# Weight sums by adding transfers: part of the weight preparation of a feed-forward stage moved from VectorE to transfers that GpSimd issues

## The chip, the cores and the metric

The kernel runs on one core of one Trainium2 chip. The metric is the device time of one execution in microseconds (us). Before the change it is 1514.25 us, the median of 2 runs (1512.74 and 1515.76).

## The reference

The program is one inference step of a two-layer transformer on 640 tokens: 512 latent tokens and 128 prompt tokens, with 1024 features each. Layer 0 mixes tokens with latent attention and neighbourhood attention, layer 1 with grouped-query attention. Each layer ends with a gated feed-forward stage of width 2816. All of it is in 32-bit floats.

```python
D_MODEL = 1024
D_FF = -(-8 * D_MODEL // (3 * 256)) * 256        # 2816

def swiglu(h, w_in, w_out):
    gate, up = jnp.split(h @ w_in, 2, axis=-1)
    return (jax.nn.silu(gate) * up) @ w_out

def reference(...):
    for l in range(DEPTH):                        # DEPTH = 2
        ...
        xp = xp + g1_p * out_p
        xs = xs + g1_s * out_s
        hp = modulate(rms_norm(xp, norm_ffn[l]), sh2_p, sc2_p)
        hs = modulate(rms_norm(xs, norm_ffn[l]), sh2_s, sc2_s)
        xp = xp + g2_p * swiglu(hp, w_ffn_in[l], w_ffn_out[l])
        xs = xs + g2_s * swiglu(hs, w_ffn_in[l], w_ffn_out[l])
```

The change concerns `h @ w_in` of layer 1: the products with the gate and up weights.

## The kernel before

**Arithmetic.** Operands of TensorE are split in two parts: a rounded high part (type fp32r) and the low part, which is the difference from the full value. A product of two split operands is three matmuls: high by high, high by low, low by high. ScalarE makes the high part of a weight tile by a copy into the fp32r type, VectorE the low part by a subtraction.

**The feed-forward stage.** `ffn(l, ...)` walks over 22 blocks of 128 of the 2816 columns. Each block fb has an up tile u and a gate tile g in memory, `wFI[l, fb, 1]` and `wFI[l, fb, 0]`, each 128 x 1024 values or 512 KB: eight pieces of 128 input features side by side, of which the first four (the left half) and the last four (the right half) are the two halves of the inner dimension. Tokens are split in two halves of 320 too. From block 2 on, gate and up of a block are computed together as a two by two block product with seven instead of eight half-products (a scheme of Strassen's kind). This needs sums of weight halves beside the weights:

- X is u itself.
- Y is s13: left half g left + g right, right half u left + g left.
- Z is s24: left half s13 right + g right, right half s24 left + u right.
- W is the right half of g.

A block makes seven half-products, each of 4 pieces by 3 matmuls, so 84 matmuls of 128x128 by 128x320. In order they are X with "11", Y with "D", W with "E" (this one belongs to the block before, the `job`), Z with "N", X with "21", Z with "22", Y with "C". The first, E, N and C write a bank g, D and 22 a bank b5, 21 a bank b2. ScalarE copies out what is in g after the first product (p1), after N (u1), and b5 after D (p5). VectorE adds these up.

**Weights ahead.** In block fb the weights of n = fb + 1 are prepared, by a class `Weights`: `sums` makes s13 and s24 in four VectorE additions of 128 x 512, `hi("X")`, `hi("Y")`, `hi("Z")` and `hi_w` the high parts on ScalarE, and `lo(...)` and `lo_w` the low parts on VectorE. The split tiles X, Y and Z take turns in six places. s13 and s24 share a tag "ws" with two places. The raw u tiles share three places with the `wm` tiles (weights of a modulation that VectorE works off in some of the blocks), the raw g tiles have two.

**What sets the order.** Nearly all VectorE work of the loop is issued through `dve` and all ScalarE work through `act`, two objects that tie each instruction behind the one issued before, so each of the two engines keeps the order of the code. The order of the transfers is not tied like that. A planner lays out the queues: a load is put where its place comes free, so that u(fb + 3) is issued in block fb, while the code names `fetch_u(fb + 2)` there. All transfers of this loop go through the queue of SyncE: u, g, `wm`, and the spills, by which finished blocks (7 tiles of 320 KB for a pair of blocks) are parked in memory. GpSimd has nothing to do in the second layer's blocks. In the trace most instructions of the loop carry the line of the helper `dve`/`act` (L1097), and all matmuls L62, so they are told apart by tile names (s is s13 or s24, wX, wY and wZ the split tiles, "wu" and "wg" the raw ones, p and u ScalarE's copies p1, p5 and u1; lead and sg the activations, hd the split activations on their way to the spills).

The stage exists for both layers; `paired` is true for layer 1.

Of the kernel before, what the change touches and what calls it, by code (L numbers as in the profile page):

```python
# [11 lines left out]
F32 = mybir.dt.float32  # L12
F32R = mybir.dt.float32r
AF = mybir.ActivationFunctionType
ALU = mybir.AluOpType
# [3 lines left out]
P = 128  # L19
# [8 lines left out]
FB = DFF // P  # L28
# [21 lines left out]
def body(ctx, tc, xT, vecs, crow, wm0, wm0g, wm1, wA, wNV, wNA, wMK, wMV, wOA, wGQ, wGK, wGV, wOC,  # L50
         wFI, wFO, cckvT, ckrT, cnkT, cnv, cgkT, cgv, rpbp, tabM, tabK, tabG, maskN,
         yT, o_ckvT, o_krT, o_nkT, o_nv, o_gkT, o_gv):
    nc = tc.nc
    V, S, G = nc.vector, nc.scalar, nc.gpsimd
# [32 lines left out]
    def bank(name, kind="m"):  # L87
        if kind == "m":
            return psp.tile([P, 512], F32, tag="m", bufs=4, name=name)
        return ypool["pool"].tile([P, 512], F32, tag=kind, bufs=ypool["tags"][kind], name=name)  # L90
# [10 lines left out]
    def tmp(name):  # L101
        return tp.tile([P, T], F32, tag="t", bufs=3, name=name)

    def f(ap):
        return ap.bitcast(F32)
# [55 lines left out]
    def load(src, n, name):  # L161
        raw = rawp.tile([P, 1024], F32, tag="raw", name=name)
        nc.sync.dma_start(raw[:, :n], src)
        return raw[:, :n]

    def after(inst, fn):
        if inst is None:
            return fn()
        with tc.issue_after(inst.ins):
            return fn()  # L170
# [901 lines left out]
    def ffn(l, x, pend, hm, nxt, side, opened):  # L1072
        ph, fk, dr, hd, fs, fp, w0, _ = opened
        paired = l == 1
# [5 lines left out]
        def room():  # L1080
            place[0] += 1
            return hd[(place[0] - 1) % len(hd)]
# [3 lines left out]
        def wtile(name):  # L1086

            turn[0] += 1
            return (wp, fp)[turn[0] % 2].tile([P, 2, 1024], F32R, tag="w", bufs=3, name=name)
# [10 lines left out]
        dve, act = Line(), Line()  # L1100


        def high(t, src):
            act(S.activation, t[:, 0, :], src, AF.Copy)

        def low(t, src):
            dve(V.tensor_tensor, t[:, 1, :], src, f(t[:, 0, :]), ALU.subtract)

        def two(t):
            return t[:, 0, :], t[:, 1, :]  # L1110
# [5 lines left out]
        def product(ps, wt, w0, which, first):  # L1116
            for k, (h, l_) in enumerate(hm.operand(which)):
                a, b = [w[:, w0 + k * P:w0 + k * P + P] for w in wt]
                mm3(ps[:, :HT], a, b, h, l_, first and k == 0, k == 3, skip_group_check=not first)

        def utile(name):
            return tp.tile([P, HT], F32, tag="u", bufs=7, name=name)
# [3 lines left out]
        def spill(fb, dh, dl):  # L1126
            if fb < FB - STAY:
                spilt[fb] = []
                for t, c in ((dh, "h"), (dl, "l")):
                    d = dr.tile([P, T], F32, name=f"sp{l}_{fb}{c}")  # L1130
                    nc.sync.dma_start(d, f(t))
                    spilt[fb].append(d)
            else:
                kept[fb] = dh, dl
# [34 lines left out]
        def fetch_u(fb):  # L1169
            if fb < FB:  # L1170
                raws[fb] = [load(wFI[l, fb, 1], 1024, f"wu{l}_{fb}r")]

        def fetch_g(fb):
            if fb == FEW:
                raws[fb].append(load(wFI[l, fb, 0], 1024, f"wg{l}_{fb}r"))
            elif fb < FB:
                rg = fp.tile([P, 1024], F32, tag="wr", bufs=2, name=f"wg{l}_{fb}r")
                nc.sync.dma_start(rg, wFI[l, fb, 0])
                raws[fb].append(rg)

        class Weights:

            def __init__(self, fb):
# [3 lines left out]

            def sums(self):
                ru, rg = self.u, self.g
                s13 = fp.tile([P, 1024], F32, tag="ws", bufs=2, name=f"s13{l}_{self.fb}")  # L1190
                dve(V.tensor_tensor, s13[:, :512], rg[:, :512], rg[:, 512:], ALU.add)
                dve(V.tensor_tensor, s13[:, 512:], ru[:, :512], rg[:, :512], ALU.add)
                s24 = fp.tile([P, 1024], F32, tag="ws", bufs=2, name=f"s24{l}_{self.fb}")
                dve(V.tensor_tensor, s24[:, :512], s13[:, 512:], rg[:, 512:], ALU.add)
                dve(V.tensor_tensor, s24[:, 512:], s24[:, :512], ru[:, 512:], ALU.add)
                self.s = {"X": ru, "Y": s13, "Z": s24}
                self.t = {c: wtile(f"w{c}{l}_{self.fb}") for c in "XYZ" if c != "X" or self.X is None}

            def hi(self, c):
                if c in self.t:  # L1200
                    high(self.t[c], self.s[c])

            def lo(self, c):
                if c in self.t:
                    low(self.t[c], self.s[c])
                    setattr(self, c, two(self.t[c]))

            def hi_w(self):
# [108 lines left out]
        for fb in range(FEW, FB):  # L1317

            first = fb < FEW + AHEAD
            n = Weights(fb + 1) if fb < FB - 1 else None  # L1320
            b5 = bank(f"fd{l}_{fb}")
            up = tmp(f"up{l}_{fb}")
            sg = lead if paired and PAIR_OF.get(fb, (0, 1))[1] == 0 else tmp(f"sg{l}_{fb}")
            both = paired and job and job[0] in PAIR_OF
            p5, u1, g2 = [utile(f"{c}{l}_{fb}") for c in ("p5", "u1", "g2")]
            if n:
                n.sums()
            if n and not first:
                n.hi("X")
            if fb in early:  # L1330
                g = early[fb][0]
            else:
                g, b2, p1 = bank(f"fg{l}_{fb}"), bank(f"fu{l}_{fb}", "y"), utile(f"p1{l}_{fb}")
                product(g, w.X, 0, 11, True)
                act(S.activation, p1, g[:, :HT], AF.Copy)
            if n and not first:
                n.hi("Y")
                n.lo("X")
                n.hi("Z")
                n.lo("Y")  # L1340
                fetch_u(fb + 2)
            after(PE.last, lambda: product(b5, w.Y, 0, "D", True))
            act(S.activation, p5, b5[:, :HT], AF.Copy)
            if n and not first:
                n.lo("Z")
            if job:
                jb, jg, jW, jup, jsg = job
                product(jg, jW, 0, "E", False)
                if jb in early:
                    dve(V.tensor_tensor, jsg[:, HT:T], jup[:, HT:T], jsg[:, HT:T], ALU.mult)  # L1350
                act(S.activation, jsg[:, 0:HT], jg[:, :HT], AF.Silu, scale=-1.0)
                if jb in early:
                    dve(V.tensor_tensor, jsg[:, 0:HT], early[jb][1], jsg[:, 0:HT], ALU.mult)
                else:
                    dve(V.tensor_tensor, jsg, jup, jsg, ALU.mult)
            if n and not first:
                n.hi_w()
            if both:
                split_pair(jb, jsg, 0)
            elif job:  # L1360
                dh, dl = room(), room()
                act(S.activation, dh, jsg, AF.Copy)
            product(g, w.Z, 0, "N", False)
            act(S.activation, u1, g[:, :HT], AF.Copy)
            if n:
                if first:
                    for c in "XYZ":
                        n.hi(c)
                        n.lo(c)
                    fetch_u(fb + 2)  # L1370
                    n.hi_w()
                n.lo_w()
                fetch_g(fb + 2)
            if both:
                split_pair(jb, jsg, 1)
            elif job:
                dve(V.tensor_tensor, dl, jsg, f(dh), ALU.subtract)
                spill(jb, dh, dl)
            if fb not in early:
                product(b2, w.X, 512, 21, True)  # L1380
                dve(V.tensor_tensor, up[:, 0:HT], b2[:, :HT], p1, ALU.add)
            if both:
                split_pair(jb, jsg, 2)
            step("fb", fb, dve)
            step("load", fb + 1, act)
            product(b5, w.Z, 512, 22, False)
            dve(V.tensor_tensor, up[:, HT:T], b5[:, :HT], u1, ALU.add)
            product(g, w.Y, 512, "C", False)
            dve(V.tensor_tensor, g2, g[:, :HT], p5, ALU.add)
            act(S.activation, sg[:, HT:T], g2, AF.Silu, scale=-1.0)  # L1390
            job, w = (fb, g, w.W, up, sg), n
# [69 lines left out]
        pss, ws = {}, {}  # L1461
# [43 lines left out]
        if paired:  # L1505
# [51 lines left out]
            for c, i in [(c, i) for c in ("T4", "T1", "B22") for i in range(len(PAIRS))][len(more):]:  # L1557
                tag = spots.pop(0)
                fetch_kind(c, i, *((fo, "hd") if tag == "fo" else (ring, tag)))
            for p in range(4):  # L1560
# [3 lines left out]
                for k, (c, which, to) in enumerate(PLAN):  # L1564
                    j = p * len(PLAN) + k
# [121 lines left out]
    ws = [unit(wGK[v], 1024, f"wgk{v}") for v in range(2)]  # L1687
# [366 lines left out]
```

## Time and profile before

| | |
|---|---|
| Time, median of 2 runs | 1514.25 us |
| Time of the profiled execution | 1513.06 us |
| Its span, from first to last instruction | 1511.3 us |
| Mean granted TensorE clock | 0.992 |
| TensorE busy | 1455.6 us, 96% of the span |
| VectorE busy | 1191.1 us, 79% |
| ScalarE busy | 760.1 us, 50% |
| GpSimd busy | 224.6 us, 15% |
| Blocks 5 to 20 of layer 1, from 1142.6 to 1339.5 us | 196.9 us, TensorE busy 196.9, VectorE 189.1, ScalarE 107.4, GpSimd 0 |
| Read from memory and written to it | 191.18 MB and 34.68 MB |

The profile is one execution. An engine's busy time counts only its own work, not waiting, and not the issuing of transfers. A share over the whole span mixes stages, so for the blocks a line of their own is given. A transfer has an issue, on the queue of an engine, and a landing some us later; only the landing releases who waits for it.

### The profile page before, as it was taken

Reading aid. Unit: us, or ns where it says so; the run is one execution under the profiler, and the core shown is the slowest. Engines: PE = TensorE matmul, PEld = TensorE weight load, DVE = VectorE, ACT = ScalarE, POOL = GpSimd, SP = SyncE. Lnnn points to the kernel's source line nnn. Section 1 sums busy time; section 2 is a strip of 40 time slices with the busy share of each in tenths; the row PEclk is TensorE's granted clock in tenths of the full one; section 3 lists DMA queues with packets and bytes.
Section 4 is the critical chain, followed back from the end, with each engine's and each line's share of the span. In section 5 each row is a group of like instructions: output and inputs, shape, how many; then the busy total and the mean of one; then the engine's idle time right before and its main releaser. Section 6 shows DMA issues by size and latency. Waiting matters only on the chain.

```text
span 1511.3 us, 25796 instructions
## 1 busy us (share of the span) xinstructions
PE 1455.6 (96%) x9856; PEld 1401.0 (93%) x9856; DVE 1191.1 (79%) x2234; ACT 760.1 (50%) x1501; POOL 224.6 (15%) x295
## 2 busy tenths in 40 slices
PE   5999989989999999999999999999999999999996
PEld 4888878879999999999999889989999999999996
DVE  5646686885899999977997777784899999953486
ACT  5435576773656554441123656673655555542242
POOL 0225544431100000000001433221200000000000
PEclk9999999999999999999999999999999999999998
DMA  9324541005155555569763210012145556669531
GB/s 373 107 104 137 184 151 46 29 15 167 57 172 184 178 185 184 179 209 332 276 218 130 90 46 29 29 57 79 57 170 185 177 191 209 214 213 313 181 95 70
DMA packets 79723, 227.54 MB, mean 151 GB/s; under 512 B 8832, under 2 KB 14224, under 8 KB 79344
## 3 DMA queue, kind: packets, MB, share of 16 engines
q1 hardware_dynamic: 77552, 222.54, 43.0%
q10 hardware_dynamic: 1632, 2.43, 0.5%
q8 instruction: 77, 1.26, 0.3%
q0 software_dynamic: 416, 0.93, 0.2%
q14 instruction: 46, 0.38, 0.1%
HBM read 191.18 MB, written 34.68 MB: 149 GB/s over the span
## 4 chain that ended last, share of the span: by engine, by line
PE 84%; DVE 8%; ACT 4%; DMA 2%; issue 2%; POOL 0%; DVEq 0%; SPq 0%; ACTq 0%; POOLq 0%
PE fg L62 20%; PE fd L62 9%; PE fo L62 7%; PE fu L62 6%; PE gq L62 2%; PE nq L62 2%; PE nk L62 2%; PE fo_2b L62 1%; PE fo_0b L62 1%; DMA mraw<-in_wm 1%; PE go L62 1%; PE fo_2a L62 1%; PE fo_0a L62 1%; PE mod L62 1%; PE ms L62 1%
## 5 line engine op out<-in xcount | busy, mean ns | idle before, releaser
L1645 DVE SCALAR_TENSOR_TENSOR junk<-wm,cb 128x1024 bf16<-128x1024 f32 x62 | 75.6, 1219 | 7.1 <-DMA wm<-in_wm 6.6
L1097 ACT ACTIVATE sg<-g 128x320 f32<-128x320 f32 x34 | 16.1, 472 | 115.0 <-DVE g L1097 115.0
L251 POOL TENSOR_SCALAR h10h<-h10t,gs,mods 128x320 fp32r<-128x320 f32 x4 | 3.6, 888 | 429.5 <-DVE h10t L245 427.8
L62 PE MATMUL gq<-h10h,wgq 128*128 128x320 f32 x256 | 65.7, 315 | 0.5 <-DVE gb L1828 0.3
L1097 DVE SCALAR_TENSOR_TENSOR junk<-wm,cb 128x1024 bf16<-128x1024 f32 x50 | 61.0, 1220 | 0.8
L1097 DVE TENSOR_TENSOR wY<-s,wY 128x1024 fp32r<-128x1024 f32 x40 | 48.8, 1219 | 2.2 <-ACT wY L1097 2.2
L1097 DVE TENSOR_TENSOR wZ<-s,wZ 128x1024 fp32r<-128x1024 f32 x40 | 48.7, 1219 | 0.0
L62 PEld LDWEIGHTS gq<-h10h,wgq 128*128 128x128 f32 x256 | 44.7, 188 | 1.8 <-PE gtp L66 1.3
L1097 ACT ACTIVATE wZ<-s 128x1024 fp32r<-128x1024 f32 x40 | 42.4, 1060 | 0.1
L1097 ACT ACTIVATE wY<-s 128x1024 fp32r<-128x1024 f32 x40 | 42.0, 1049 | 0.0
L1829 ACT ACTIVATE gp<-gs,gb,rq 128x640 f32<-128x640 f32 (+1 forms) x40 | 31.9, 797 | 20.0 <-DVE gb L1828 15.9
L62 PE MATMUL gq<-h10l,wgq 128*128 128x320 f32 x128 | 39.4, 308 | 0.0
L62 PE MATMUL fg<-h11E,wW 128*128 128x320 f32 x240 | 38.7, 310 | 0.0
L62 PE MATMUL fg<-h01q,wX 128*128 128x320 f32 x240 | 38.6, 309 | 0.0
L62 PE MATMUL fg<-h11q,wX 128*128 128x320 f32 x240 | 38.6, 309 | 0.0
L62 PE MATMUL fg<-h01N,wZ 128*128 128x320 f32 x240 | 38.6, 309 | 0.0
L62 PE MATMUL fg<-h11N,wZ 128*128 128x320 f32 x240 | 38.6, 309 | 0.0
L62 PE MATMUL fu<-h11q,wX 128*128 128x320 f32 x240 | 38.6, 308 | 0.0
L62 PE MATMUL fu<-h01q,wX 128*128 128x320 f32 x240 | 38.6, 309 | 0.0
L62 PE MATMUL fg<-h01E,wW 128*128 128x320 f32 x240 | 38.6, 309 | 0.0
L62 PE MATMUL fd<-h01q,wZ 128*128 128x320 f32 x240 | 38.5, 309 | 0.0
L62 PE MATMUL fg<-h11C,wY 128*128 128x320 f32 x240 | 38.5, 309 | 0.0
(3209 smaller groups left out, 5257.5 us busy)
## 6 DMA issues: line engine op xcount, KB each, us to landing
wm<-in_wm SPq DMA_DIRECT2D x48, 512.0 KB, 3.9
mraw<-in_wm SPq DMA_DIRECT2D x24, 512.0 KB, 3.6
mraw<-in_wm SPq DMA_DIRECT2D x8, 1024.0 KB, 15.3
hr_T<-sp_T SPq DMA_DIRECT2D x21, 320.0 KB, 5.7
hr_B<-sp_B SPq DMA_DIRECT2D x18, 320.0 KB, 6.0
wm<-in_wm0g SPq DMA_DIRECT2D x8, 512.0 KB, 3.4
x<-in_xT SPq DMA_DIRECT2D x8, 320.0 KB, 5.6
xr<-in_xT SPq DMA_DIRECT2D x8, 320.0 KB, 6.0
```

The lines of the kernel that those rows point to most:

```text
L62: cls.last = nc.tensor.matmul(*a, **k)
L251: G.tensor_scalar(h[:, c0:c1], t, self.gsl[:, k, 0:1], self.ml[:, self.sh + k, 0:1], ALU.mult, ALU.add)
L1097: self.last = after(self.last, lambda: op(*a, **k))
L1645: def step(kind, at, line=lambda op, *a, **k: op(*a, **k)):
L1829: S.activation(dst, src, AF.Exp, bias=nb, scale=rq[:, j:j + 1], accum_out=ll[:, j:j + 1])
```

## The change

In layer 1, for blocks 7 to 21:

- s13 is no longer made by two VectorE additions. A new function `fetch_s(fb + 2)`, called in block fb ahead of `fetch_u(fb + 2)`, loads the left half of g and the left half of u into the two halves of an s13 tile, by two transfers of 256 KB on SyncE's queue. Two more transfers of 256 KB, issued by GpSimd, add the right half of g and the left half of g at their destination.
- The low part of X is no longer made by VectorE's subtraction. ScalarE writes the negated high part into the place of the low part, as one more `act` right behind `hi("X")`, and a transfer of 512 KB, issued by GpSimd, adds the raw u from memory to it.

The raw tiles of u and g are still loaded, for X's high part, for s24 and for W. s13 keeps its tag "ws" with two places, which it shares with s24.

```diff
+        ADDED = 6
+        summed = {}
+
+        def fetch_s(fb):
+            if paired and ADDED < fb < FB:
+                s13 = fp.tile([P, 1024], F32, tag="ws", bufs=2, name=f"s13{l}_{fb}")
+                for j in range(2):
+                    nc.sync.dma_start(s13[:, 512 * j:512 * j + 512], wFI[l, fb, j][:, :512])
+                for j in range(2):
+                    nc.gpsimd.dma_start(s13[:, 512 * j:512 * j + 512], wFI[l, fb, 0][:, 512 - 512 * j:1024 - 512 * j],
+                                        accum_op=ALU.add)
+                summed[fb] = s13
+
         class Weights:
...
             def sums(self):
                 ru, rg = self.u, self.g
-                s13 = fp.tile([P, 1024], F32, tag="ws", bufs=2, name=f"s13{l}_{self.fb}")
-                dve(V.tensor_tensor, s13[:, :512], rg[:, :512], rg[:, 512:], ALU.add)
-                dve(V.tensor_tensor, s13[:, 512:], ru[:, :512], rg[:, :512], ALU.add)
+                if self.fb in summed:
+                    s13 = summed.pop(self.fb)
+                else:
+                    s13 = fp.tile([P, 1024], F32, tag="ws", bufs=2, name=f"s13{l}_{self.fb}")
+                    dve(V.tensor_tensor, s13[:, :512], rg[:, :512], rg[:, 512:], ALU.add)
+                    dve(V.tensor_tensor, s13[:, 512:], ru[:, :512], rg[:, :512], ALU.add)
...
             def hi(self, c):
                 if c in self.t:
                     high(self.t[c], self.s[c])
+                    if c == "X" and paired and self.fb > ADDED:
+                        hi, lo = two(self.t[c])
+                        act(S.activation, lo, f(hi), AF.Copy, scale=-1.0)
+                        nc.gpsimd.dma_start(lo, wFI[l, self.fb, 1], accum_op=ALU.add)
+                        self.added = True
+
+            added = False
 
             def lo(self, c):
                 if c in self.t:
-                    low(self.t[c], self.s[c])
+                    if c != "X" or not self.added:
+                        low(self.t[c], self.s[c])
                     setattr(self, c, two(self.t[c]))
...
                 n.hi("Z")
                 n.lo("Y")
+                fetch_s(fb + 2)
                 fetch_u(fb + 2)
```

## The prediction

> **What bounds the kernel now.** I read the page first, then a table of busy times over the second layer's blocks, then the timeline of one block, then the transfers.
>
> ```profile
> span 1511.3 us, 25796 instructions
> PE 1455.6 (96%) x9856; PEld 1401.0 (93%) x9856; DVE 1191.1 (79%) x2234; ACT 760.1 (50%) x1501; POOL 224.6 (15%) x295
> ```
>
> ```profile
> core 0: us, PE busy (x) PEld busy (x) DVE busy (x) ACT busy (x) POOL busy (x), PEclk, DMA share, GB/s
> 1142.60:1339.50 196.90, 196.90 (x1346) 196.90 (x1345) 189.10 (x298) 107.43 (x192) 0.00 (x0) 1.00 0.57 192
> ```
>
> The first fence is the page's head. In the second, from the table of busy times, the line under the heads covers the sixteen blocks fb = 5 to 20, in which all that the change touches runs. TensorE is busy for all of its 196.9 us at the full granted clock: 12.31 us a block. VectorE is busy for 96% of the time, ScalarE for 55%, GpSimd not at all. The transfer engines are busy for 0.57 of it at 192 GB/s, so about 337 GB/s when they work. Nothing that leaves VectorE can shorten this stretch, since TensorE waits for nothing in it; the change can only be free or cost something. One block (fb = 10, which prepares the weights of n = 11) looks like this; the columns are start, duration, engine and line, and what is written from what.
>
> ```profile
> 1204.02 1.92 PE L62 MATMUL fg<-h11q,wX 128*128 128x320 f32 x12
> 1204.22 0.49 DVE L1097 TENSOR_TENSOR g<-fg,p 128x320 f32<-128x320 f32 x1
> 1204.63 0.68 DVE L1097 TENSOR_TENSOR s<-wg_11r 128x512 f32<-128x512 f32 x1
> 1204.81 0.47 ACT L1097 ACTIVATE lead<-g 128x320 f32<-128x320 f32 x1 [2.49 <-DVE g L1097]
> 1205.18 1.04 ACT L1097 ACTIVATE wX<-wu_11r 128x1024 fp32r<-128x1024 f32 x1
> 1205.23 0.68 DVE L1097 TENSOR_TENSOR s<-wu_11r,wg_11r 128x512 f32<-128x512 f32 x1
> ...
> 1205.95 0.69 DVE L1097 TENSOR_TENSOR s<-s,wg_11r 128x512 f32<-128x512 f32 x1
> 1206.13 0.42 ACT L1097 ACTIVATE p<-fg 128x320 f32<-128x320 f32 x1
> 1206.45 1.05 ACT L1097 ACTIVATE wY<-s 128x1024 fp32r<-128x1024 f32 x1
> 1206.67 0.69 DVE L1097 TENSOR_TENSOR s<-s,wu_11r 128x512 f32<-128x512 f32 x1
> 1207.28 1.22 DVE L1097 TENSOR_TENSOR wX<-wu_11r,wX 128x1024 fp32r<-128x1024 f32 x1
> ...
> 1207.39 1.06 ACT L1097 ACTIVATE wZ<-s 128x1024 fp32r<-128x1024 f32 x1
> ...
> 1208.42 1.22 DVE L1097 TENSOR_TENSOR wY<-s,wY 128x1024 fp32r<-128x1024 f32 x1
> 1208.53 0.33 SPq L163 DMA_DIRECT2D wu_13r<-in_wFI  x1
> ...
> 1209.55 1.22 DVE L1097 TENSOR_TENSOR wZ<-s,wZ 128x1024 fp32r<-128x1024 f32 x1
> ...
> 1210.68 0.82 DVE L1097 TENSOR_TENSOR lead<-up,lead 128x640 f32<-128x640 f32 x1
> ...
> 1211.54 0.47 ACT L1097 ACTIVATE hd_1l<-lead 128x320 fp32r<-128x320 f32 x1 [1.03 <-DVE lead L1097]
> 1211.92 0.42 ACT L1097 ACTIVATE u<-fg 128x320 f32<-128x320 f32 x1
> ...
> 1214.57 1.92 PE L62 MATMUL fg<-h11C,wY 128*128 128x320 f32 x12
> ...
> 1216.33 1.93 PE L62 MATMUL fg<-h11q,wX 128*128 128x320 f32 x12
> ```
>
> From here on, times with a plus sign are us after the block's start at 1204.02. The reader should see two deadlines. At +12.31 the next block multiplies with X, whose low part is read by the third matmul, at about +12.6. At +10.55 product C writes the bank from which ScalarE's copy into "u" reads, so that copy must have ended; it ends at +8.3.
>
> **What is removed.** Per block two sums of 0.68 us and X's subtraction of 1.22 us leave VectorE: 2.6 us, 39 us over fifteen blocks. TensorE hid all of it: worth 0.
>
> **What is added on ScalarE.** One copy of 128x1024, as the row of wX 1.04 us, between X's rounding and "p". It pushes the following copies back by up to 1.05 us; ScalarE idles 45% of the stretch, and "u" has 2.2 us of room: 0. Without that room it would be 15 x 1.05 = 16 us.
>
> **X's low part.** Rounding ends at +2.2, the negated copy at +3.25. GpSimd then issues the adding transfer of 512 KB. The trace has GpSimd issues and transfers, but none that adds:
>
> ```profile
> 859.53 0.59 POOL L1741 DMA_DIRECT2D out_o_gkT<-kn  x1
> ```
>
> ```profile
> out_o_gkT<-kn POOLq DMA_DIRECT2D x2, 64.0 KB, 2.8
> ...
> wu_13r<-in_wFI SPq DMA_DIRECT2D x1, 512.0 KB, 3.5
> wg_13r<-in_wFI SPq DMA_DIRECT2D x1, 512.0 KB, 4.4
> sp_T<-hd_1h SPq DMA_DIRECT2D x2, 320.0 KB, 4.7
> sp_B<-hd_0h SPq DMA_DIRECT2D x1, 320.0 KB, 3.4
> ...
> cb<-in_crow SPq DMA_DIRECT2D x1, 1024.0 KB, 5.3
> ```
>
> The first fence is from GpSimd's timeline, the second from the view of transfers, whose last column is us from issue to landing. With 0.6 us for the issue the add is under way from about +3.9 and has 8.7 us. Its bounds are 3.5 (a quiet plain load of its size, wu) and 10.6 (twice the 1024 KB row, cb). I take 5.3, one cb: every destination byte must be read as well as the addend, so 512 KB added means 1024 KB read. It lands near +9: 0, and at the upper bound 1.9 us late in each of fifteen blocks, 28 us.
>
> **The sums: a new loop.** Today s13(n) is made by VectorE where it is used. After the change it is loaded into one of two "ws" slots, which it shares with s24. The slot for s13(n+1) is the one that s13(n) leaves, when Y's subtraction has read it. So the loads wait on SyncE for VectorE. Queued behind them there are u, g and the spills; SyncE stands behind VectorE today as well, and u and g come more than 12 us early (u of block 13 is issued in block 10, and block 12 splits it), so that wait itself costs 0. GpSimd's two adds wait for the loads, the next block's s24 waits for the adds, and the next Y's subtraction follows s24. That closes a ring from block to block:
>
> From the landing of s13 to the slot's release: two s24 sums (0.69 + 0.69), Y's subtraction 1.22, signals about 0.05: 2.65 us (Y's rounding, 1.05, fits beside the sums).
>
> From the release to the next landing, call it R: signal 0.1; the two loads of 256 KB, together the bytes of one wg, 4.4 (bounds 3.5 and 5.3); signal 0.1; the second add's issue 0.6; the adds, 1024 KB read, 5.3 as cb, plus 0.65 because in every second block they run into the larger group of spills (320 KB took 4.7 instead of 3.4, so 1.3 in every second block). R = 11.15. From below: 0.1 + 3.5 + 0.1 + 0.6 + 2.8 = 7.1, if an add costs no more than a 64 KB write by GpSimd. From above: 0.1 + 5.3 + 0.1 + 0.6 + 10.6 = 16.7. The values taken are those of rows of the same size in the same stretch or stage.
>
> The ring takes 2.65 + 11.15 = 13.8 us against a block of 12.31, so s13 comes 1.49 us later in each block than in the one before. What is late next: s13's arrival holds VectorE's and ScalarE's fixed order, and through it "u". After arrival: 1.38 for s24, 1.22 for Y, 1.22 for Z, 0.82 for the multiplication into lead, one or two roundings of 0.47 and 0.42 for "u", with signals 5.6 to 6.0. Against product C at +10.55 s13 may come by about +4.5. The first one, s13(7), is released in block 5 by Y(6)'s subtraction (as in the row, ending at +5.62) and comes at 5.62 + 11.15 - 12.31 = +4.46 of block 6. The allowance is used up at once, and the fourteen steps to s13(21) cost TensorE 14 x 1.49 = 20.9 us. Where s13 comes by about +3.35, Y's subtraction is held by ScalarE instead and ends at +6.0; so R up to 9.65 costs nothing.
>
> **Transfers.** By the table, 0.57 x 12.31 = 7.0 us of a block are in use; 512 KB of plain loads add 524 KB / 337 GB/s = 1.6, and the adds of 1024 KB 3.1 if they cost as loads: 11.7 of 12.31, just room. That is why I keep the upper values for the range.
>
> **Sum.** The profiled execution took 1513.06 us (span 1511.3 and 1.8 around it), 1.2 below the median of 1514.25. 1513.06 + 20.9 = **1534 us**.
>
> **The rivals.**
>
> *The adds stay hidden.* If R is at most 9.65, nothing changes: 1512 to 1519. For it: a quiet 512 KB lands in 3.5 us, GpSimd is idle, and bursts of loads leave gaps in every block. With 3.5 for the loads and 4.4 for the adds R is 8.7. Against it: a transfer that reads its destination can't be quicker than a plain one, and the heavy blocks stretch plain ones already. The Trainium skill, "DMA: Bandwidth & Descriptors", section "Anatomy of one DMA — SWDGE (gpsimd) path", gives about 2.0 us plus the bytes at 436 GB/s; as my estimate 3.2 us for 512 KB added, by which R is 8.4 and the change is free. The wu row (3.5) is near to that for a plain load; no row shows an add. Chance 0.29.
>
> *The transfer engines become the bound.* If an add occupies them for two loads, a block needs 7.0 + 1.6 + 6.2 = 14.8 us, 2.5 more than TensorE: 15 x 2.5 = 37, 1550. For three loads 17.9 us: 84, 1597; it decides from 1.2 loads up. For it: a share of 0.57 before. Against it: the share counts waiting too, and spills can move into gaps. The Trainium skill, "Collectives: The Full Stack", section "The bandwidth ceiling: the fold count and why AG ≠ RS ≠ AR", has an adding transfer at about half a copy's rate, because it reads two sources through one ring; that is the case of two loads, and no row here can test it. Chance 0.17.
>
> *GpSimd's order.* If the planner puts X's add behind the next sums' adds, it waits for their loads: released at +6.0, landed at +10.5, two issues, then its own: under way at +12.3, landed at +16.6 to +17.6 against +12.6. 4 to 5 us in fifteen blocks: 1573 to 1588. For it: the engine serves one queue in order. Against it: X's add is ready 7 us earlier. Chance 0.10.
>
> *Faster*: only if TensorE's pace hides a dependence on VectorE's load; the row of full occupancy at clock 1.00 speaks against it. Chance 0.02, at most a few us.
>
> **How the numbers follow.** The forecast, a ring of 12.7 to 15 us, has 0.42: R from 10 to 12.4, 1517 to 1553. What a measurement of this kernel can tell from no change is about 2%, 30 us, so up to 1544.5; R above 11.9 crosses it, which I give 0.13 of the 0.42. Slower: 0.13 + 0.17 + 0.10 = 0.40. Same: 0.29 + 0.29 = 0.58. Faster: 0.02. Low end 1512 from the hidden case; the high end 1592 takes in the forecast, the order case and the transfer bound up to nearly three loads, and leaves out about 0.15. The forecast's own range is 1517 to 1553.
>
> **What would show it.** Right: in blocks 6 to 20 VectorE idles before s24 for a transfer, the ScalarE copy "u" ends just before product C, and TensorE has gaps ahead of C that sum to some 20 us, with blocks of about 13.8 us. Hidden: blocks of 12.31 with VectorE's busy share near 0.75. Transfer bound: a transfer share above 0.9 and late spills, u and g too. Order: TensorE waits ahead of the first product, for wX. I am wrong if an adding 256 KB lands in under 4 us or over 8, or if the slot of s13 is not the one that I named.

## The result, and the profile after

| | before | after |
|---|---|---|
| Time, median of 2 runs | 1514.25 us | 1568.24 us (1567.03 to 1569.45) |
| Time of the profiled execution | 1513.06 us | 1569.45 us |
| Its span | 1511.3 us | 1567.7 us |

The changed kernel takes 1.0357 times as long, with a 95% interval of 1.03 to 1.0413. That is 54 us more by the medians and 56.4 us by the spans. The forecast was 21 us more, by a ring of transfers and sums that takes longer than a block. The sign and the mechanism were right, the size was not: the time lies within the whole range of 1512 to 1592 us, but outside the 1517 to 1553 that the ring was given, and the chances had favoured no change that could be told (0.58) over slower (0.40).

The head of the page of the changed kernel:

```profile
span 1567.7 us, 25971 instructions
PE 1469.4 (94%) x9856; PEld 1407.4 (90%) x9856; DVE 1158.0 (74%) x2189; ACT 777.0 (50%) x1516; POOL 262.9 (17%) x340
```

VectorE has 33 us less to do (1191.1 to 1158.0), which is what the change set out to move, and the span is 56 us longer. The table of busy times shows where; the stretch runs from the start of block 6 to the end of block 20, fifteen blocks:

```profile
core 0: us, PE busy (x) PEld busy (x) DVE busy (x) ACT busy (x) POOL busy (x), PEclk, DMA share, GB/s
1152.90:1395.30 242.40, 200.59 (x1262) 192.24 (x1261) 143.38 (x236) 116.91 (x195) 38.79 (x45) 0.96 0.90 243
```

A block now takes 242.4 / 15 = 16.16 us instead of 12.31. TensorE, which was busy all the time, works for 13.37 us of each and waits for the rest. VectorE, 0.96 busy before, is at 0.59: the new bound is no engine. The chain of waits says what it is. These are its pieces in order of time in blocks 10 and 11 (start, duration, what the time was spent on):

```profile
1217.46 8.42 DMA s<-in_wFI
...
1225.90 0.70 DVE s L1097
...
1227.23 1.23 DVE wY L1097
...
1228.48 3.87 DMA s<-in_wFI
...
1232.92 0.46 POOL s L1190
...
1233.45 7.81 DMA s<-in_wFI
...
1241.29 0.70 DVE s L1097
```

This is the ring that the prediction described, link by link: adds land, s24's first sum, Y's subtraction (written wY), the loads of the next s13 (3.87), GpSimd's issue, the adds (7.81), the next sum. In this turn it is 8.37 us from the adds' first issue to the sum (1232.92 to 1241.29), less than the mean of 9.18 that is used below. The same ring on the timeline, with the two products of TensorE that wait for it; block 10 starts at 1218.07:

```profile
1225.90 0.69 DVE L1097 TENSOR_TENSOR s<-s,wg_11r 128x512 f32<-128x512 f32 x1 [5.79 <-DMA s<-in_wFI]
...
1227.23 1.22 DVE L1097 TENSOR_TENSOR wY<-s,wY 128x1024 fp32r<-128x1024 f32 x1
...
1228.48 1.09 SPq L1188 DMA_DIRECT2D s<-in_wFI  x2
...
1228.78 2.03 PE L62 MATMUL fd<-h11q,wZ 128*128 128x320 f32 x12 [1.76 <-ACT p L1097]
...
1231.28 2.03 PE L62 MATMUL fg<-h11C,wY 128*128 128x320 f32 x12 [0.47 <-ACT u L1097]
...
1232.92 1.75 POOL L1190 DMA_DIRECT2D s<-in_wFI  x2 [9.05 <-DVE up L1097]
...
1239.19 0.86 POOL L1221 DMA_DIRECT2D wX<-in_wFI  x1 [4.52 <-ACT p L1097]
```

In the kernel before, s24's first sum started 1.93 us after the block's start; here at +7.83, after a wait of 5.79 us for the transfer. GpSimd issues X's add behind s13's, at 1239.19, and in this stretch nothing waits for it.

From the view of waits of the stretch (engine and line, what it waited for; us in total, times, longest):

```profile
DVE s L1097 <- DMA s<-in_wFI: 94.0, 15, 8.0
...
PE fd L62 <- ACT p L1097: 32.5, 15, 4.1
...
PE fg L62 <- ACT u L1097: 7.1, 11, 0.8
...
PE fg L62 <- ACT p L1097: 2.2, 4, 0.6
```

Fifteen times VectorE waits for the adds, and fifteen times TensorE then waits for ScalarE's copies, mostly ahead of the product just before C (32.5 us), less ahead of C (7.1 us). The three rows of TensorE make 41.8 us, which is 242.4 - 200.59; the rest of the loss, 15 x 1.06, is that TensorE runs longer on the same products after a wait (the last section).

The view of transfers (the last column is us from issue to landing):

```profile
s<-in_wFI SPq DMA_DIRECT2D x30, 256.0 KB, 3.9
s<-in_wFI POOLq DMA_DIRECT2D x30, 256.0 KB, 8.0
wX<-in_wFI POOLq DMA_DIRECT2D x15, 512.0 KB, 6.6
```

An adding transfer of 256 KB takes 8.0 us, twice the plain load of the same size. Two of them are under way at a time, as the two loads are. Last, the first and the last of the fifteen sums that start the ring's turns, and what stands ahead of the first: Y's subtraction for n = 6 and the start of block 6.

```profile
1146.63 1.22 DVE L1097 TENSOR_TENSOR wY<-s,wY 128x1024 fp32r<-128x1024 f32 x1
...
1152.93 1.92 PE L62 MATMUL fg<-h11q,wX 128*128 128x320 f32 x12
...
1161.90 0.69 DVE L1097 TENSOR_TENSOR s<-s,wg_7r 128x512 f32<-128x512 f32 x1 [6.93 <-DMA s<-in_wFI]
...
1387.81 0.69 DVE L1097 TENSOR_TENSOR s<-s,wg_21r 128x512 f32<-128x512 f32 x1 [5.51 <-DMA s<-in_wFI]
```

Between the last two lie fourteen turns: 225.91 / 14 = 16.14 us a turn. Fourteen times 16.14 - 12.31 is 53.6 us, and the first late sum makes TensorE wait 3.6 us in block 6. Together 57, against a difference of the spans of 56.4.

### The profile page after: what moved, and what is told of

Read it like the earlier page. It is cut to its first block, busy times and chain, and to the rows that moved or that the text cites. A ratio compares the mean times of both kernels' runs of the same rounds, so it can differ in the third digit from the quotient of the medians.

```text
span 1567.7 us, 25971 instructions
## 1 busy us (share of the span) xinstructions
PE 1469.4 (94%) x9856; PEld 1407.4 (90%) x9856; DVE 1158.0 (74%) x2189; ACT 777.0 (50%) x1516; POOL 262.9 (17%) x340
## 4 chain that ended last, share of the span: by engine, by line
PE 67%; DVE 12%; DMA 11%; ACT 6%; issue 3%; POOL 1%; DVEq 0%; SPq 0%; ACTq 0%; POOLq 0%
PE fg L62 13%; DMA s<-in_wFI 9%; PE fo L62 7%; PE fd L62 5%; PE fu L62 4%; PE gq L62 2%; PE nk L62 2%; PE nq L62 1%; DVE s L1097 1%; PE fo_2b L62 1%; PE fo_0b L62 1%; PE go L62 1%; PE fo_2a L62 1%; PE fo_0a L62 1%; PE mod L62 1%
## 5 line engine op out<-in xcount | busy, mean ns | idle before, releaser
L62 PE MATMUL fd<-h11q,wZ 128*128 128x320 f32 x240 | 45.0, 342 | 32.5 <-ACT p L1097 32.5
L62 PEld LDWEIGHTS fd<-h11q,wZ 128*128 128x128 f32 x240 | 39.8, 209 | 36.4 <-ACT p L1097 36.4
L1190 POOL DMA_DIRECT2D s<-in_wFI x30 | 26.5, 1030 | 211.8 <-DVE up L1097 147.0
L62 PE MATMUL fg<-h11C,wY 128*128 128x320 f32 x240 | 42.6, 330 | 7.1 <-ACT u L1097 7.1
L62 PEld LDWEIGHTS fg<-h11C,wY 128*128 128x128 f32 x240 | 38.6, 203 | 10.5 <-ACT u L1097 10.5
L1854 ACT ACTIVATE gp<-gs,gb,rq 128x640 f32<-128x640 f32 (+1 forms) x40 | 31.9, 797 | 20.0 <-DVE gb L1853 15.9
L62 PEld LDWEIGHTS fg<-h11N,wZ 128*128 128x128 f32 x240 | 35.9, 188 | 3.3 <-ACT p L1097 3.3
```

What stands on the lines that cost most here:

```text
L62: cls.last = nc.tensor.matmul(*a, **k)
L1190: nc.gpsimd.dma_start(s13[:, 512 * j:512 * j + 512], wFI[l, fb, 0][:, 512 - 512 * j:1024 - 512 * j], accum_op=ALU.add)
L1854: S.activation(dst, src, AF.Exp, bias=nb, scale=rq[:, j:j + 1], accum_out=ll[:, j:j + 1])
```

## The experiments

"Before" is the kernel before, run on the same chip beside each group. Where a turn of the ring is given, it is worked out as above, from the start of s24's first sum in the first turn and in the last.

**X's add alone (x_only).** The sums are made by VectorE again, and only X's low part comes by an adding transfer:

```diff
-            if paired and ADDED < fb < FB:
+            if False and paired and ADDED < fb < FB:
```

> Only X's low part is made by the adding transfer; s13 is made by VectorE as before. Ring theory (the slot of s13 closes a ring of about 16 us from block to block): there is no ring left, and X's add has 8.7 us until the third matmul of the next block, against 6.6 us from issue to landing in the changed kernel: 1511 to 1518 us, blocks of 12.31 us. Rival, transfer engines full: work of 7.0 + 3 = 10 us a block, also below 12.31, 1511 to 1518. If X's add is part of the loss (late for the next block): TensorE waits ahead of a block's first product, over 1525.

1513.54 us against 1513.23, ratio 1.0004 (0.9995 to 1.0014). The transfers, and the busy times of blocks 6 to 20:

```profile
wX<-in_wFI POOLq DMA_DIRECT2D x15, 512.0 KB, 7.2
```

```profile
1154.80:1339.50 184.70, 184.36 (x1256) 183.91 (x1256) 161.02 (x266) 113.65 (x195) 13.04 (x15) 1.00 0.85 235
```

The add takes 7.2 us, more than the 5.3 I had put in, and still has room: TensorE is busy for 184.36 of 184.70 us. X's part is free. It is no gain either: VectorE's busy time fell from 0.96 to 0.87 of the stretch and nobody was waiting for it.

**The sums alone (sums_only).** s13 comes by adding transfers, X's low part is VectorE's:

```diff
-                    if c == "X" and paired and self.fb > ADDED:
+                    if False and c == "X" and paired and self.fb > ADDED:
```

> Only s13 comes by adding transfers; X's low part is VectorE's subtraction again. Ring theory: the subtraction of X lies between s24 and Y's subtraction, so the hold grows from 2.55 to 3.7 us; with R unchanged at 12.5 to 13.6 the ring is 16.2 to 17.3 us and the time 1560 to 1580. If R is long only because X's add shares the engines with the sums' adds, R falls to about 11 and the ring to 14.7: 1545. Rival, transfer engines full: work of 7.0 + 1.6 + 3.1 = 11.7 us a block fits into 12.31: 1511 to 1520.

1583.78 us, ratio 1.0476 (1.0458 to 1.0494): slower than the whole change by 15 us, and a little above what I expected.

```profile
1166.99 0.69 DVE L1097 TENSOR_TENSOR s<-s,wg_7r 128x512 f32<-128x512 f32 x1 [6.56 <-DMA s<-in_wFI]
...
1404.20 0.69 DVE L1097 TENSOR_TENSOR s<-s,wg_21r 128x512 f32<-128x512 f32 x1 [4.59 <-DMA s<-in_wFI]
```

```profile
1166.90:1404.20 237.30, 195.38 (x1166) 187.32 (x1165) 149.66 (x237) 94.92 (x170) 24.59 (x28) 0.91 0.71 204
```

The first fence is from its timeline: a turn is 16.94 us. The second, from its table of busy times, covers the same fourteen turns: the transfer engines are busy for only 0.71 of the time, and the kernel is slower than with 0.90. So the loss is not that they are full. The turn is longer because X's subtraction of 1.22 us now stands between the sums and Y's subtraction: the place of s13 is held for 3.69 us instead of 2.55, while the path from release to landing is about the same (13.25 instead of 13.58). The step from the adds' issue to the sum is 9.00 us without X's add and 9.18 with it, so X's add is not what makes it long.

**The ring cut open (free_places).** All three moves stay, but s24 takes no "ws" place: its halves are written over the left half of the raw g and the right half of the raw u, which have been read for the last time. s13 has both places to itself, and its loads need not wait for Y's subtraction of the block before.

```diff
-                s24 = fp.tile([P, 1024], F32, tag="ws", bufs=2, name=f"s24{l}_{self.fb}")
-                dve(V.tensor_tensor, s24[:, :512], s13[:, 512:], rg[:, 512:], ALU.add)
-                dve(V.tensor_tensor, s24[:, 512:], s24[:, :512], ru[:, 512:], ALU.add)
+                if paired and self.fb > ADDED:
+                    s24 = rg[:, :512], ru[:, 512:]
+                    dve(V.tensor_tensor, s24[0], s13[:, 512:], rg[:, 512:], ALU.add)
+                else:
...
             def hi(self, c):
...
+                    if c == "X" and paired and self.fb > ADDED:
+                        a, b = self.s["Z"]
+                        dve(V.tensor_tensor, b, a, b, ALU.add)
...
```

> All three moves stay, but s24 gives up its places: for blocks 7 to 21 its halves are written over the left half of the raw g and the right half of the raw u, and both places of ws belong to s13, so that its loads and adds can run one block ahead. VectorE and ScalarE have one instruction more each per block. Ring theory: the ring is gone, 1511 to 1520, blocks of 12.31 us. Rival, transfer engines full (an add occupies them for two loads): 14.5 us a block whatever the places, 1545 to 1555, transfer share near 1.

1524.77 us, ratio 1.007 (1.005 to 1.009), above the 1511 to 1520 that I expected and far below the rival's 1545. All but 11.5 of the 54 us are gone, with the same adds by the same engine. TensorE's waits that are left:

```profile
PE fg L62 <- DMA wX<-in_wFI: 4.6, 8, 1.5
PE fd L62 <- ACT p L1097: 3.3, 1, 3.3
```

The copy p is late once, instead of fifteen times, and now X's add is late in eight blocks. It lands in 9.1 us here and is due early in the next block. Blocks 7 to 20, those behind the first late one, with the columns as above:

```profile
1171.48:1350.59 179.11, 174.53 (x1178) 172.41 (x1177) 134.05 (x236) 108.75 (x198) 33.32 (x39) 1.00 1.02 302
```

They take 179.11 / 14 = 12.79 us each, with the transfers of the change under way: 54 MB at 302 GB/s, where as many blocks of the changed kernel move 55 MB at 243. So the transfer engines can do this work in 12.79 us a block, and they are not what made a block take 16.16. The share of 1.02 also says that this column is packet time and no fraction of what the engines can do.

**The same without X's add (free_sums).** As free_places, with X's low part by VectorE; the second half of s24 is then made behind that subtraction, which is the last to read the raw u.

```diff
-                    if c == "X" and paired and self.fb > ADDED:
-                        hi, lo = two(self.t[c])
-                        act(S.activation, lo, f(hi), AF.Copy, scale=-1.0)
-                        nc.gpsimd.dma_start(lo, wFI[l, self.fb, 1], accum_op=ALU.add)
-                        self.added = True
...
```

> As free_places (both places of ws for s13, s24 over the raw halves), but X's low part is VectorE's subtraction again. If what was left of the loss there (11.5 us) is X's add, landing late because the transfer engines are full: 1511 to 1517, no wait for wX. If it came from the extra instructions or from the sums' adds: 1520 or more.

1519.05 us against 1512.44, ratio 1.0049 (1.003 to 1.0068), a little above the 1511 to 1517 that I expected, and no wait for wX is left. Its timeline in block 6:

```profile
1167.39 2.85 PE L62 MATMUL fd<-h11q,wZ 128*128 128x320 f32 x12 [4.22 <-ACT p L1097]
1170.57 2.53 PE L62 MATMUL fg<-h11C,wY 128*128 128x320 f32 x12 [0.33 <-ACT u L1097]
```

These are TensorE's only two waits in the blocks, 4.5 us. The two products behind them take 2.85 and 2.53 us instead of 1.92, another 1.5. The sum, 6.0, is the whole difference of the spans (1517.3 to 1511.3). So only the first s13 was late: for n = 7 its place is still that of block 6's sums, which had their s24 in "ws".

**The first turn too (free_early).** As free_sums, but s24 leaves "ws" one block earlier, here and wherever the same condition stands:

```diff
-                if paired and self.fb > ADDED:
+                if paired and self.fb >= ADDED:
```

> As free_sums, but s24 leaves its places from block 6 on, one block before the first added sum, so that the place of s13(7) is free a block earlier. If what was left in free_sums is only the first sum coming late (one wait of 4.2 us and a slow product behind it): no wait of TensorE in the blocks, 1510 to 1516, ratio 0.998 to 1.002. If the sums' adds cost something in every block: still 1518 to 1520.

1512.09 us against 1512.11, ratio 1.0004 (0.9993 to 1.0015). Busy times, and the adds in the view of transfers:

```profile
1154.80:1339.50 184.70, 184.70 (x1262) 184.70 (x1261) 160.44 (x265) 103.44 (x197) 23.64 (x27) 1.00 0.90 274
```

```profile
s<-in_wFI POOLq DMA_DIRECT2D x30, 256.0 KB, 7.9
```

The sums' adds are as slow as ever, 7.9 us, the transfer engines' share is 0.90 as in the changed kernel, and TensorE never waits. For the sums, the wait was made by the ring alone. This kernel has no X's add; the same early start with X's add was not run, and 5 to 7 us could remain of it: free_places is 11.5 us above before where free_sums is 6.6, and its blocks 7 to 20 lose 14 x 0.48 us. free_early is no faster than the kernel before, though VectorE has 9% of the stretch less to do: TensorE's 12.31 us a block was the bound.

**What an add costs by itself (probe).** In the kernel before, adds and plain loads by GpSimd into an unused raw tile, at two quiet places of layer 1's attention, in one run; each waits for the one ahead of it, but for the two adds of the pair.

```diff
...
+            nc.sync.dma_start(probe, src)
+            nc.gpsimd.dma_start(probe, src, accum_op=ALU.add)
+            for j in range(2):
+                nc.gpsimd.dma_start(probe[:, 512 * j:512 * j + 512], src[:, 512 * j:512 * j + 512], accum_op=ALU.add)
+            nc.gpsimd.dma_start(probe, src)
+            nc.gpsimd.dma_start(probe[:, :512], src[:, :512], accum_op=ALU.add)
+            nc.gpsimd.dma_start(probe[:, :512], src[:, :512])
```

> The kernel before, with a few extra transfers into an unused tile at two quiet places of layer 1's attention: a plain 512 KB load on SyncE, then by GpSimd one after the other an add of 512 KB, two adds of 256 KB side by side, a plain 512 KB, an add of 256 KB, a plain 256 KB. If an add's own cost made R long: the pair of adds lands in 7 to 8 us also here, the 512 KB add in over 6. If sharing the engines did: the pair in 4 to 5.5 us and the 512 KB add in about 5. A plain 512 KB by GpSimd should land in 3.5 to 4.5.

GpSimd's timeline at the second place. From the start of one row to the start of the next is the cost of the first, issue included:

```profile
883.07 0.89 POOL L1872 DMA_DIRECT2D probe<-in_wFI  x1 [1.25 <-issue]
889.15 0.89 POOL L1874 DMA_DIRECT2D probe<-in_wFI  x1 [3.56 <-DMA probe<-in_wFI]
890.53 1.21 POOL L1874 DMA_DIRECT2D probe<-in_wFI  x1
895.85 0.59 POOL L1875 DMA_DIRECT2D probe<-in_wFI  x1 [3.68 <-DMA probe<-in_wFI]
900.32 0.88 POOL L1876 DMA_DIRECT2D probe<-in_wFI  x1 [1.44 <-DMA probe<-in_wFI]
904.85 0.59 POOL L1877 DMA_DIRECT2D probe<-in_wFI  x1 [2.03 <-DMA probe<-in_wFI]
```

In order: one add of 512 KB takes 6.1 us; the pair of adds of 256 KB, as s13's, 6.7; a plain load of 512 KB 4.5; one add of 256 KB 4.5. The other place gave 6.0, 6.9, 4.8 and 4.6. The pair lies a little below the 7 to 8 us of the first expectation, so an add's own cost is the larger part. Even undisturbed the pair costs 6.7 to 6.9, where my sum had 0.6 + 5.3 = 5.9 ahead of the 0.65 for the spills. In the changed kernel the mean from the first issue to the next sum is 9.18: 2.3 to 2.5 us are company, that is, other transfers under way at the same time.

**Without reading the destination (plain_gp).** The two s13 transfers of GpSimd overwrite instead of adding.

```diff
-                    nc.gpsimd.dma_start(s13[:, 512 * j:512 * j + 512], wFI[l, fb, 0][:, 512 - 512 * j:1024 - 512 * j],
-                                        accum_op=ALU.add)
+                    nc.gpsimd.dma_start(s13[:, 512 * j:512 * j + 512], wFI[l, fb, 0][:, 512 - 512 * j:1024 - 512 * j])
```

> The changed kernel, but the two transfers that GpSimd issues for s13 overwrite instead of adding (so the sums are wrong); same bytes from memory, same queue, same places, and X's add stays. In the quiet measurement the pair of adds took 6.8 us and a plain 512 KB by GpSimd 4.6. If reading the destination is what makes the step long: issue to landing of the pair falls from 9.2 to 5.5 to 6.5 us, the ring from 16.1 to 12.5 to 13.4, time 1520 to 1532. If the GpSimd queue or the meeting with spills and g's load is what makes it long, whatever the kind: it stays near 8.5 to 9 us and the time above 1555.

1547.3 us against 1512.44, ratio 1.0228 (1.0207 to 1.0248), between the two expectations.

```profile
1162.80 0.69 DVE L1097 TENSOR_TENSOR s<-s,wg_7r 128x512 f32<-128x512 f32 x1 [6.64 <-DMA s<-in_wFI]
...
1366.57 0.69 DVE L1097 TENSOR_TENSOR s<-s,wg_21r 128x512 f32<-128x512 f32 x1 [5.83 <-DMA s<-in_wFI]
```

A turn is 14.55 us and the step from issue to sum 7.05 instead of 9.18. That the two transfers add is worth 2.1 us of it; up to 0.65 of these are GpSimd's longer issue of a pair, 1.75 us instead of 1.10. The turn is shorter by only 1.6 us, since the path from release to the adds' issue takes 4.95 here instead of 4.40. Even plain transfers in that place cost 35 us: the greater part of the price is a second transfer that starts when the first has landed, the smaller that it adds.

**Without the spills (no_spills).** The paired blocks' spills are left out; the tiles that stand in for them are written ahead of the stage, by `park`.

```diff
...
-            d = dr.tile([P, T], F32, name=f"sp{l}_{kind}{i}")
-            solo[kind, i] = t, d
+            solo[kind, i] = t, parked[kind, i]
...
-            nc.sync.dma_start(d, f(t))
...
+    park(op[2], x[0])
```

> The changed kernel without the spills of the paired blocks (the 21 parked tiles are written once with other data on ScalarE's queue ahead of the stage, so the output is wrong). If the adds take 9.2 us instead of the quiet 6.8 because the spills run at the same time: the step falls to 7 to 7.5 us, the ring to 13.9 to 14.4, time 1535 to 1545. If not the spills but X's add, g's load or the adds themselves: it stays at 8.5 to 9 us and the time at 1558 to 1568.

1567.23 us, ratio 1.0359 (1.0338 to 1.0381). By itself the total would speak for the second expectation, but writing the stand-ins delays the whole stage; the ring shows the effect:

```profile
1177.83 0.69 DVE L1105 TENSOR_TENSOR s<-s,wg_7r 128x512 f32<-128x512 f32 x1 [6.66 <-DMA s<-in_wFI]
...
1384.02 0.69 DVE L1105 TENSOR_TENSOR s<-s,wg_21r 128x512 f32<-128x512 f32 x1 [5.41 <-DMA s<-in_wFI]
```

The first sum is 15.9 us later than in the changed kernel, and the fourteen turns take 206.2 us instead of 225.9: 14.73 a turn, and 7.46 from issue to sum. The step is as expected, the turn a little longer than the 13.9 to 14.4. The spills are 1.7 of the 2.4 us of company. From n = 10 to n = 19, the step is 7.5 to 8.4 in the five turns in which the load of wm runs as well, and 6.2 to 6.8 in the five in which it doesn't, which is no more than the quiet price. In these five the load of g and X's add run as in the changed kernel, so neither lengthens the step here.

**From block 14 only (from_14).** Eight late sums, so seven turns.

```diff
-        ADDED = 6
+        ADDED = 13
```

> The change for blocks 14 to 21 only. Ring theory: each step of the ring loses 16.1 - 12.3 = 3.8 us, and the first late arrival some 4; eight sums have seven steps: 1513 + 4 + 7 x 3.8 = 1543 to 1546, with blocks of 12.31 up to fb = 12. If the loss were a one-off or a matter of the whole stretch (clock, start): near 1560 or below 1525.

1543.39 us, ratio 1.0202 (1.0181 to 1.0222), as expected.

The first sum for n = 14 starts at 1247.54 and that for n = 21 at 1359.74, so a turn is 112.2 / 7 = 16.03 us, and the blocks ahead of it keep their 12.31. The loss grows with the number of turns, as a ring's must.

**One add for two (one_add).** The loads bring the right half of g and the left half of u, and one add of 512 KB puts the left half of g, read twice, on both.

```diff
-                for j in range(2):
-                    nc.sync.dma_start(s13[:, 512 * j:512 * j + 512], wFI[l, fb, j][:, :512])
-                for j in range(2):
-                    nc.gpsimd.dma_start(s13[:, 512 * j:512 * j + 512], wFI[l, fb, 0][:, 512 - 512 * j:1024 - 512 * j],
-                                        accum_op=ALU.add)
+                nc.sync.dma_start(s13[:, :512], wFI[l, fb, 0][:, 512:])
+                nc.sync.dma_start(s13[:, 512:], wFI[l, fb, 1][:, :512])
+                gl = wFI[l, fb, 0][:, :512]
+                nc.gpsimd.dma_start(s13.rearrange("p (a b) -> p a b", a=2),
+                                    bass.AP(tensor=gl.tensor, offset=gl.offset, ap=[gl.ap[0], [0, 2], gl.ap[1]]),
+                                    accum_op=ALU.add)
```

> The changed kernel, ring and X's add included, but the two adds of a sum are one transfer of 512 KB: the loads bring the right half of g and the left half of u, and one add puts the left half of g, read twice, on both. Ring theory with the step as measured: one issue of 0.86 us instead of two and a quiet add of 5.8 instead of 6.8 us take about 1 us out of R, and fourteen steps bring 14 us: 1551 to 1557. If the engines' work sets the time and not the chain, the bytes are the same: 1565 to 1570.

1582.55 us against 1512.11, ratio 1.0469 (1.0448 to 1.049): I expected a gain on the changed kernel and got a loss of 14 us more.

```profile
1164.63 0.69 DVE L1097 TENSOR_TENSOR s<-s,wg_7r 128x512 f32<-128x512 f32 x1 [7.50 <-DMA s<-in_wFI]
...
1399.85 0.69 DVE L1097 TENSOR_TENSOR s<-s,wg_21r 128x512 f32<-128x512 f32 x1 [7.49 <-DMA s<-in_wFI]
```

A turn is 16.80 us. From the loads' issue to the add's it takes 5.16 us instead of 4.37, since one add waits for both loads; and from there 9.06, hardly less than the 9.18 of the pair. The first number is the wait for the second load: in the turn of the changed kernel shown above, GpSimd is released by the landing of the first load at 1232.35, and the second lands some 0.6 us later. The second number, against a quiet 6.0 for one add and 6.7 for a pair, I can only explain by guess: two adds run beside each other, and one add has no such overlap. That its source is read twice could also be it; no run tells the two apart.

All of them by the ring. The third column is the turns times what a turn takes above 12.31; what the time has beyond it is mostly the first late sum (block 6 takes 17.17 us in sums_only, 18.43 in one_add), and in no_spills the late start as well. The first row doesn't show it, though block 6 takes 16.48 us there: the fifteen blocks lose 57.7 us and the span 56.4, while the medians, of two runs each, differ by 54.0:

| kernel | turn, us | turns x (turn - 12.31) | time above before |
|---|---|---|---|
| the change | 16.14 | 14 x 3.83 = 53.6 | 54.0 |
| sums_only | 16.94 | 14 x 4.63 = 64.8 | 70.6 |
| one_add | 16.80 | 14 x 4.49 = 62.9 | 70.4 |
| plain_gp | 14.55 | 14 x 2.24 = 31.4 | 34.9 |
| from_14 | 16.03 | 7 x 3.72 = 26.0 | 31.0 |
| no_spills | 14.73 | 14 x 2.42 = 33.9 | 54.8, of which 15.9 late start |
| free_early | no ring | 0 | 0.0 |

## Why the prediction was right in kind and wrong in size

**VectorE's relief is worth 0.** Right. x_only and free_early take work from VectorE without any wait and gain nothing.

**ScalarE's copy and X's low part cost 0.** Right, though the add took 7.2 us alone and 6.6 in the change where I put 5.3. In free_places, at 9.1, it came late eight times, which cost 5 to 7 us; I had put its price at 0 and at 28 us for an add of 10.6.

**The ring.** Right, link by link, and three runs show it: the sums' adds outside a ring cost nothing (free_early), a longer hold of the place makes a longer turn (sums_only), and half the turns cost half as much (from_14). The hold is 2.55 (2.65 predicted), from release to the adds' first issue 4.40 (4.6 predicted).

**The adds in the ring, "the adds, 1024 KB read, 5.3 as cb, plus 0.65".** This is the term that failed. With the issue I had 6.55 us; measured are 9.18. The links ahead of it were 0.2 shorter, so R is 13.58 instead of 11.15 and a turn 16.14 instead of 13.8. The excess of a turn over a block, 1.49 predicted, is a difference of two large numbers: 2.4 us too little in R made it 3.83, and the loss of the fourteen turns 53.6 us instead of 20.9. R is within the bounds of 7.1 to 16.7 that I had worked out, but the range of the ring went only up to 12.4. Of the 2.6 us that the term lacks, the pair's own price is 0.8 to 1.0: 5.9 by the cb row, 6.7 to 6.9 by the probe. So one plain load of twice the size was too low a price for two adds, and that 6.55 meets the quiet price nearly is luck, since it held 0.65 for company. The other 1.7 are company. The load of g for a later block and the spills of finished blocks wait for VectorE as the loads of s13 do, and they run beside the adds in every turn, not only in every second: in fourteen of the fifteen turns the load of g is issued 1.2 to 2.6 us ahead of the adds, and in each of them two or more spills are issued between 2 us ahead of them and 4 us behind. I had charged the spills 0.65 us in the mean; they cost 1.7, and the rest, by the turns of no_spills wm's load, some 0.7.

**The first s13.** Predicted at +4.46 of block 6, measured at 1161.90 - 1152.93 = +8.97. Of the 4.51 us, 2.90 are R (14.05 in that turn). The other 1.61 come from taking block 5 to be like block 10: Y's subtraction for n = 6 ends 5.08 us ahead of block 6's start, where block 10's ended 12.31 - 5.62 = 6.69 ahead. Its cost is the first wait of TensorE, 3.6 us, which I had at 0.

**Where TensorE waits.** I named the copy "u" and product C. The greater wait stands one product earlier, for the copy p (32.5 us, against 7.1 for u). Both copies stand behind the late sum in ScalarE's order, but the sign I told the reader to look for was the smaller of the two.

**The rivals.** "The adds stay hidden" fell with R at 13.58 against 9.65. The estimate beside it, 3.2 us for 512 KB added, from the Trainium skill, "DMA: Bandwidth & Descriptors", section "Anatomy of one DMA — SWDGE (gpsimd) path", doesn't hold here: the probe has 6.0 and 6.1, and 4.5 to 4.8 for a plain load of that size, from one issue to the next. "GpSimd's order" did not come up: X's add waits for no sum. "The transfer engines become the bound" foresaw a share of 0.9 or more and an add at two loads' price, and both came true; its 1550 was even nearer to the time than my 1534. But sums_only is the slowest with 0.71, and free_places does nearly the same transfers in 12.79 us a block, where this rival had 14.8. So full engines are not the cause; company lengthens the turn, and the turn is what costs. My sign of being wrong, an add of 256 KB over 8 us, stands at its edge: the median is 8.0.

## What to carry to other kernels

A tile that is loaded, then added to in place, and whose place is freed by work that waits for the tile before it, closes a ring: add up all its links and compare the sum with the pace of the loop, however idle the engines are. Where ring and loop are near to each other, the loss is a small difference of large numbers, so price each link from transfers in the same company, above all those that the same event releases. Freeing the place one round earlier, here by writing s24 over raw tiles that are done, took the whole price of the sums away; and work taken from an engine that nobody waits for is worth nothing, even where it is made free.

## What the runs showed of the hardware

**What an adding transfer occupies.** The view of queues of the changed kernel, for the fifteen blocks (packets, MB, share of the 16 engines' time):

```profile
q1 hardware_dynamic: 17065, 43.04, 52.8%
q0 software_dynamic: 6480, 15.73, 36.6%
```

q0 holds the adds: 15.73 MB in 0.366 x 242.4 = 88.7 us, 177 GB/s. The plain transfers of q1 move 43.04 MB in 128 us, 336 GB/s. By packet time, a byte added took 1.9 times as long as a byte copied; in the other kernels whose transfers on q0 all add, the same division gives 1.7 to 2.1. In plain_gp, where the pair for s13 only copies, q0 moves 14.45 MB in 66.0 us; with X's adds taken at 177 GB/s, my estimate for the copies is 290 GB/s, so by this estimate most of the difference is the adding, and not GpSimd's queue. The Trainium skill, "Collectives: The Full Stack", section "The bandwidth ceiling: the fold count and why AG ≠ RS ≠ AR", has transfers that add at about half the rate of those that copy; these rows agree. GpSimd's issue is longer as well, 0.88 us against 0.59 for a plain one in the probe.

**TensorE's clock falls after the waits.** From the timeline of the changed kernel, three products that waited and one that follows, and the stretch of the second in the table of busy times, with the columns as above:

```profile
1164.78 2.03 PE L62 MATMUL fd<-h11q,wZ 128*128 128x320 f32 x12 [2.90 <-ACT p L1097]
...
1182.50 3.57 PE L62 MATMUL fd<-h11q,wZ 128*128 128x320 f32 x12 [4.13 <-ACT p L1097]
1185.87 2.55 PE L62 MATMUL fg<-h11C,wY 128*128 128x320 f32 x12
...
1278.04 2.44 PE L62 MATMUL fd<-h11q,wZ 128*128 128x320 f32 x12 [2.65 <-ACT p L1097]
```

```profile
1182.50:1186.10 3.60, 3.60 (x13) 3.60 (x14) 3.40 (x5) 1.85 (x4) 0.00 (x0) 0.50 0.81 273
```

After a wait of 4.13 us the granted clock is 0.50 for 3.6 us, and the product takes 3.57 instead of 1.92 us. The Trainium skill, "TensorE: Matmul & The Clock Gate", section "Part 1: The HAM clock gate (the "warmup" mystery)", has half the clock after an idle window of some 3.4 us; in this trace the product was also slow after a wait of 2.65 us, and not after one of 2.90. In the ring it should cost little, since the next turn is late anyway, which no run shows by itself; in free_sums, with a single late sum, it was 1.5 of the 6.0 us.

**Left open.** That the 0.7 us of company beside the spills is wm's load rests on comparing turns with and without it in no_spills; no run leaves that load out. The whole change with an early start, X's add included, was not run either.
